# Seven instead of five of sixteen units by Strassen's scheme, with two weight sums made by accumulating transfers

## The chip, the cores and the metric

The kernel runs on one core of a Trainium2 chip. A core has five engines that work side by side, each with its own queue of instructions: TensorE (PE in the profile: matmuls, and PEld: the loads of its stationary operand), VectorE (DVE), ScalarE (ACT), GpSimd (POOL) and SyncE (SP), which here only issues transfers. Sixteen DMA engines carry the transfers. Engines wait for one another through semaphores. Operands lie in SBUF (128 partitions); matmuls write to PSUM, in banks of 128 x 512 float32.

The metric is the time of one execution on the device, in microseconds (us); of several runs the median is taken.

## What is computed

A small encoder of four layers on 256 tokens of width 1024, in float32. Layer i uses token mixer i mod 3: retention, a convolution module, stick-breaking attention, and retention again. After each mixer stands a feed-forward part with the square of a ReLU, and that part is what the change touches:

```python
def squared_relu_mlp(xn, w1, w2):
    h = jax.nn.relu(xn @ w1)
    return (h * h) @ w2

for i in range(DEPTH):              # 4
    ...
    x = x + m                       # m: the mixer of the layer
    x = x + squared_relu_mlp(rms_norm(x, norm_ffn[i]), ffn_w1[i], ffn_w2[i])
return rms_norm(x, final_norm)
```

w1 is 1024 x 4096 and w2 is 4096 x 1024 in each layer. The second product, (h * h) @ w2, is the "second feed-forward product" of this text: 256 tokens, an inner dimension of 4096, 1024 output columns.

## The kernel before

**Products.** Every float32 operand x is split in two: a part hi in the fast matmul type and the rest lo = x - hi. A product a b is three matmuls: a_hi b_hi, a_hi b_lo and a_lo b_hi (`triple`, L687 to L691; its matmul is L689).

**Weights.** All weights come from one array, cut into units of 128 x 1024 and, two units at a time, into chunks of 128 x 2048 (1 MB). `PLAN` (L67 to L107) lists the units in the order of their use. `unit_hi` (L336) loads the next chunk from SP's queue (L348) into one of three `raw` tiles and copies a unit to its hi part on ScalarE (L362, tile `wh`); `unit_lo` (L366) makes the rest on VectorE (L369, tile `wl`). There are five tiles each of `wh` and `wl`. Every unit goes through this conversion, so a chunk's `raw` tile comes free when its last reader is done.

**The second feed-forward product** (`down`, L684). The inner dimension falls into 16 units of 256 rows (kb). For each, the inner 256 rows are two blocks (kk), the tokens are two blocks (t), and the columns are two halves (c); the results stand in four PSUM banks C[t, c]. A plain unit makes all 8 block products, 24 matmuls. The units in `FAST` (L59) use Strassen's scheme in its variant with 7 block products, 21 matmuls. That scheme needs sums on both sides:

- of the activations: s1 to s4, made in `act` (L628, sums at L644 to L646) when the unit's columns of the first product are ready, and split into hi and lo (L652, L653). A unit's sums fill two tiles of 128 x 512. For the first two fast units they lie in `big` tiles, for the other three in `z` tiles, which up to then hold the operand of the first product.
- of the weights: with b11, b21, b12, b22 the four quarters of the chunk, t1 = b11 + b12, t3 = b12 + b22, t2 = t1 + b22 and t4 = t2 + b21. `fast_unit` (L373) makes all four on VectorE (L385), in temporaries (`tmp`, a pool of ten tiles), and converts b22 and the four sums in halves of 512 columns (L392 on ScalarE, L393 on VectorE).

Three of the seven products go to C directly, four to banks of their own (p1, p5, p7, p6; tile `mis`), and after the last mixed unit a few VectorE additions bring these to C.

**Order.** `MIXED` (L60) is the order of the first 12 units: plain and fast ones mixed. `REST` (L61) are the last four units, all plain, first for column half 0 and then for half 1, so that half 0 can be taken out while half 1 is computed. The first product runs over 16 pairs p of 256 columns (`ffn`, L623); pair p becomes the activations of unit kb = p. In the last layer `final` (L829) takes the place of `middle`: it loads the final gain into two `z` tiles (L832) and scales the rows.

Inside most stages the order of instructions on each engine comes from a planner that runs the program against a model of the machine: it gives out the tiles of a pool as they come free, in the order of the instructions that first write them, and puts in the semaphores.

**Other users.** The retention layers (0 and 3) need decay factors, 4 x 384 columns of a constant tile `cst`, loaded from SP's queue in layer 0 while the chunks 6 to 9 are loaded (`DST`, L31, L352 to L354) and used at L1006. GpSimd's queue holds 36 transfers in layer 0 (L898), sums of squares, additions of the convolution layer and a few memsets.

Of the kernel before, what the change touches and what calls it, by code (L numbers as in the profile page):

```python
# [21 lines left out]
RH = 4  # L22
DK = 256
# [7 lines left out]
DST = 6  # L31
# [27 lines left out]
FAST = (5, 6, 13, 14, 15)  # L59
MIXED = (0, 5, 1, 2, 6, 3, 13, 4, 14, 7, 15, 8)  # L60
REST = (9, 10, 11, 12)  # L61
# [48 lines left out]
NCHUNK = NUNIT // UPC  # L110

# [131 lines left out]
class Trunk:  # L243
    def __init__(self, ctx, tc, xT, w, prm, cst, fin, gn, out):
# [24 lines left out]
        self.cst = self.cp.tile([P, NCCOL], F32, name="cst", tag="cst")  # L269
# [66 lines left out]
    def unit_hi(self, key):  # L336
# [3 lines left out]
        if o == 0:  # L340
            n = self.un // UPC
            if n < len(self.first):
                self.rawt = self.first[n]
            else:
                self.rawt = self.raw.tile([P, RAWW], F32, name=self.nm("raw"), tag="raw")
                h = 1024 if n < 4 else UPC * 1024
                for a in range(0, UPC * 1024, h):
                    nc.sync.dma_start(self.rawt[:, a : a + h], self.w_d[n][:, a : a + h])  # L348
            for _ in range(min(2, len(self.later))):
                self.later.pop(0)()  # L350
            i = self.un // UPC - DST
            if 0 <= i < RH:  # L352
                n = CCOL["D"] + i * 384
                self.tc.keep_in_program_order(nc.sync.dma_start(self.cst[:, n : n + 384], self.cst_d[:, n : n + 384]))  # L354
# [18 lines left out]
    def fast_unit(self, name, l, kb):  # L373
        nc = self.nc
        ah, al = self.unit((name, l, "a", kb, 0))
        o = self.un % UPC * 1024
        assert PLAN[self.un] == (name, l, "a", kb, 512) and o
        self.un += 1
        b11, b21, b12, b22 = (self.rawt[:, n * 512 : (n + 1) * 512] for n in range(4))
        t1, t2, t3, t4 = (self.tmp() for _ in range(4))  # L380
        out = [(ah[:, :512], al[:, :512]), (ah[:, 512:], al[:, 512:])]
        h = None
        for n, (dst, x, y) in enumerate(((None, b22, None), (t1, b11, b12), (t3, b12, b22), (t2, t1, b22), (t4, t2, b21))):
            if dst is not None:
                nc.vector.tensor_add(dst, x, y)  # L385
            else:
                dst = x
            if n % 2 == 0:
                h = self.wp.tile([P, 1024], F32R, name=self.nm("wh"), tag="wh")
                g = self.wp.tile([P, 1024], F32R, name=self.nm("wl"), tag="wl")  # L390
            c = slice(n % 2 * 512, (n % 2 + 1) * 512)
            nc.scalar.copy(h[:, c], dst)  # L392
            nc.vector.tensor_sub(g[:, c], dst, h[:, c])  # L393
            out.append((h[:, c], g[:, c]))
        return out
# [227 lines left out]
    def ffn(self, i, nxt):  # L623
        nc = self.nc
        last = nxt is None
        h, rb, fast = [], [], {}

        def act(ps):  # L628
# [12 lines left out]
            if p in FAST:  # L641
# [5 lines left out]
                n = 2 * FAST.index(p) - 4  # L647
                hi, lo = (
                    self.bigt(F32R) if n < 0 else self.zp.tile([P, 512], F32R, name=self.nm("z"), tag=f"z{n + o}")
                    for o in range(2)  # L650
                )
# [32 lines left out]
    def down(self, i, h, fast, begin, hook):  # L684
# [51 lines left out]

        if i == 0:
# [91 lines left out]
    def final(self, i, h, fast):  # L829
        nc = self.nc  # L830
        self.table("sqrt_and_others")
        gain = [self.zp.tile([P, 512], F32, name=self.nm("gain"), tag=f"z{6 + c}") for c in range(2)]  # L832
        for c in range(2):
            nc.sync.dma_start(gain[c], self.fin_d[:, c * 512 : (c + 1) * 512])
# [11 lines left out]
        def hook(C, at):  # L846
            if at:
                return
# [53 lines left out]
    def retention(self, j, nxt):  # L902
# [72 lines left out]
        for h in range(RH):  # L975
# [27 lines left out]
            for t, (c0, c1) in enumerate(((0, S), (S, S + P))):  # L1003
                nc.vector.scalar_tensor_tensor(
                    out=a[t], in0=ps[:, c0:c1], scalar=ck[:, t * 4 + h : t * 4 + h + 1],
                    in1=self.c("D", c1 - c0, h * 384 + c0), op0=ALU.mult, op1=ALU.mult,  # L1006
# [751 lines left out]
```

## Time and profile before

| | |
|---|---|
| median of three runs | 1330.02 us (1329.91 to 1332.01) |
| the profiled execution: time / span | 1329.23 us / 1327.5 us |
| granted TensorE clock | 1.00 |
| TensorE busy, matmuls / weight loads | 1316.6 / 1133.6 us |
| VectorE / ScalarE / GpSimd busy | 1063.9 / 860.1 / 154.1 us |
| moved by DMA | 253.95 MB, 191 GB/s on average |

The span runs from the first to the last instruction of the profiled execution; the rest of its time lies around it. "Busy" is the sum of the listed durations of an engine's instructions. In the rows of the profile, L689 is line 689 of the kernel, an arrow stands between output and input tiles, and "<-ACT wh L362" names what ended a wait. SPq and POOLq are the queues of transfers issued by SP and GpSimd; "us to landing" is the time from a transfer's issue to its end.

The layers' feed-forward parts lie at 178 to 386 us (layer 0), 460 to 664, 750 to 957 and 1117 to the end; in each, the first product takes some 115 us and the second some 80.

### The profile page before, as it was taken

To read this page: it belongs to the slowest core of one execution; us is meant where nothing else is said; L and a number is where in the kernel's file an instruction comes from. 1 tells how busy PE (TensorE), PEld (TensorE's weight loads), DVE (VectorE), ACT (ScalarE), POOL (GpSimd) and SP (SyncE) were. 2 spreads that over 40 slices of the span, in tenths; PEclk is the share of its full clock that TensorE was granted. 3 is DMA by queue.
4 is the path that set the end of the run, shared out by engine and by line. 5 is a ranking of instruction groups with operands and counts; after the bars stand their busy time and mean duration, and the time that the engine had idled before them with its cause. 6 is when DMAs were issued, how large, how long until landed. Compare 5 with 4: busy or idle time off the path is not lost.

```text
span 1327.5 us, 20237 instructions
## 1 busy us (share of the span) xinstructions
PE 1316.6 (99%) x7703; PEld 1133.6 (85%) x7703; DVE 1063.9 (80%) x1805; ACT 860.1 (65%) x1407; POOL 154.1 (12%) x169
## 2 busy tenths in 40 slices
PE   9999999999999999999999999999999999999998
PEld 8988888888899898888888898888888888888886
DVE  7987877779778688798788588798798776798985
ACT  7555546886566478766668678866675555567663
POOL 3554411000009110000000010000020000100000
PEclk9999999999999999999999999999999999999999
DMA  8666655545765655545453355555454554555552
GB/s 312 211 218 223 227 206 191 190 159 201 277 240 152 202 182 193 188 161 220 158 189 130 127 193 189 190 190 210 169 193 171 189 180 160 206 202 191 177 192 94
DMA packets 46049, 253.95 MB, mean 191 GB/s; under 512 B 5376, under 2 KB 10112, under 8 KB 18560
## 3 DMA queue, kind: packets, MB, share of 16 engines
q1 hardware_dynamic: 43360, 245.32, 52.4%
q0 software_dynamic: 1728, 4.72, 0.9%
q10 hardware_dynamic: 864, 2.62, 0.6%
q8 instruction: 60, 0.98, 0.3%
q14 instruction: 37, 0.30, 0.1%
HBM read 245.99 MB, written 6.65 MB: 190 GB/s over the span
## 4 chain that ended last, share of the span: by engine, by line
PE 96%; DVE 2%; ACT 1%; DMA 0%; issue 0%
PE acc L577 22%; PE acc L689 19%; PE acc L573 11%; PE acc L1107 6%; PE acc L1109 6%; PE acc L1108 6%; PE mis L689 3%; PE acc L557 3%; PE acc L558 3%; PE acc L559 3%; PE mis L577 2%; PE acc L1275 1%; PE mis L573 1%; PE acc L1408 1%; DVE wl L393 1%; DVE t L385 1%
## 5 line engine op out<-in xcount | busy, mean ns | idle before, releaser
L369 DVE TENSOR_TENSOR wl<-raw,wh 128x1024 fp32r<-128x1024 f32 (+1 forms) x420 | 512.5, 1231 | 122.1 <-ACT wh L362 119.1
L362 ACT CAST wh<-raw 128x1024 fp32r<-128x1024 f32 (+1 forms) x420 | 433.2, 1041 | 232.4 <-PE acc L689 68.6
L577 PE MATMUL acc<-z,wh 128*128 128x512 f32 x1152 | 399.4, 393 | 0.0
L573 PE MATMUL acc<-z,wl 128*128 128x256 f32 x1152 | 317.6, 280 | 0.0
L689 PE MATMUL acc<-wh,big 128*128 128x512 f32 x800 | 255.9, 391 | 0.0
L577 PEld LDWEIGHTS acc<-z,wh 128*128 128x128 f32 x1152 | 214.2, 187 | 47.1
L573 PEld LDWEIGHTS acc<-z,wl 128*128 128x128 f32 x1152 | 216.9, 189 | 2.4 <-DVE t L602 0.3
L689 PEld LDWEIGHTS acc<-wh,big 128*128 128x128 f32 x800 | 150.2, 188 | 30.7
L689 PE MATMUL acc<-wl,big 128*128 128x512 f32 x400 | 156.2, 390 | 0.5 <-DVE wl L369 0.5
L1107 PE MATMUL acc<-wh,z 128*128 128x512 f32 x352 | 138.6, 394 | 0.0
L1109 PE MATMUL acc<-wh,z 128*128 128x512 f32 x352 | 137.3, 390 | 0.0
L1108 PE MATMUL acc<-wl,z 128*128 128x512 f32 x352 | 137.2, 390 | 0.0
L601 ACT COPY t<-acc 128x256 f32<-128x256 f32 x154 | 53.1, 371 | 57.3 <-PE acc L577 55.4
L689 PEld LDWEIGHTS acc<-wl,big 128*128 128x128 f32 x400 | 75.1, 188 | 17.6 <-DVE wl L369 1.8
L1107 PEld LDWEIGHTS acc<-wh,z 128*128 128x128 f32 x352 | 66.1, 188 | 15.2 <-issue 2.2
L1109 PEld LDWEIGHTS acc<-wh,z 128*128 128x128 f32 x352 | 66.1, 188 | 14.8 <-issue 0.8
L1108 PEld LDWEIGHTS acc<-wl,z 128*128 128x128 f32 x352 | 66.1, 188 | 13.3
L602 DVE TENSOR_TENSOR t<-acc,t 128x256 f32<-128x256 f32 x154 | 59.7, 419 | 17.9 <-ACT t L601 16.0
L392 ACT CAST wh<-t 128x512 fp32r<-128x512 f32 x80 | 47.1, 619 | 35.2 <-DVE t L385 12.3
L557 PE MATMUL acc<-z,wh 128*128 128x256 f32 x224 | 63.7, 284 | 0.0
L492 POOL TENSOR_TENSOR t<-t,t 128x512 f32<-128x512 f32 x15 | 24.2, 1612 | 339.1 <-ACT t L487 308.7
L558 PE MATMUL acc<-z,wh 128*128 128x256 f32 x224 | 63.4, 283 | 0.0
(300 smaller groups left out, 2098.6 us busy)
## 6 DMA issues: line engine op xcount, KB each, us to landing
raw<-in_w SPq DMA_DIRECT2D x214, 1024.0 KB, 4.9
strip<-st POOLq DMA_DIRECT2D x36, 128.0 KB, 4.0
big<-strip SPq DMA_DIRECT2D x18, 256.0 KB, 5.9
big<-in_gn SPq DMA_DIRECT2D x16, 256.0 KB, 5.3
raw<-in_w SPq DMA_DIRECT2D x7, 512.0 KB, 7.4
raw<-hd SPq DMA_DIRECT2D x8, 263.0 KB, 5.2
raw<-hd SPq DMA_DIRECT2D x8, 131.5 KB, 3.6
wh<-in_w ACTq DMA_DIRECT2D x2, 512.0 KB, 6.3
```

The source lines that it names most:

```text
L362: nc.scalar.copy(hi[:, s], src[:, s])
L369: self.nc.vector.tensor_sub(lo[:, s], src[:, s], hi[:, s])
L557: nc.tensor.matmul(o, wh[:, kk, cs], ah, start=st, stop=False, **kw)
L558: nc.tensor.matmul(o, wh[:, kk, cs], al, start=False, stop=False, **kw)
L573: mm = nc.tensor.matmul(ps[m][:, :S], wl[:, kk, cs], a[:, :S], start=first and kk == 0, stop=False, **kw)
L577: nc.tensor.matmul(ps[m], wh[:, kk, cs], a, start=False, stop=last and kk == 3, **kw)
L601: nc.scalar.copy(o[:, s], ps[m][:, S:])
L602: nc.vector.tensor_add(o[:, s], ps[m][:, :S], o[:, s])
L689: mm = nc.tensor.matmul(o, l, r, start=start and n == 0, stop=stop and n == 2, skip_group_check=True)
L1107: nc.tensor.matmul(ps[t], zh[:, s], wh[:, kk], start=k == 0, stop=False, skip_group_check=True)
L1108: nc.tensor.matmul(ps[t], zh[:, s], wl[:, kk], start=False, stop=False, skip_group_check=True)
L1109: nc.tensor.matmul(ps[t], zl[:, s], wh[:, kk], start=False, stop=k == 7, skip_group_check=True)
```

## The change

Units 9 and 12 become fast, so that 7 of 16 units use the scheme; the order of the twelve mixed units is new, with 9 next to 12 and 13 next to 14, and the last four are 7, 8, 10 and 11.

In `fast_unit` two of the four weight sums are no longer made by VectorE. SP's queue loads b12 a second time, into a temporary (t3). GpSimd's queue then issues two transfers that add what they bring to what stands at their destination: b11 onto the chunk's own b12, which makes t1 in place, and b22 onto t3. VectorE still makes t2 and t4. Since t1 and b22 are now next to each other in the chunk, they are converted together, as 1024 columns.

The activation sums of seven units need room: the third pair of tiles takes over the place of the decay factors (`room`, the same tag as `decay`), the other four take all eight `z` tiles. So the decay factors leave `cst` for a tile of their own and are loaded a second time in layer 3, and the final gain is loaded into `big` tiles, after the additions that follow the mixed units.

```diff
-FAST = (5, 6, 13, 14, 15)
-MIXED = (0, 5, 1, 2, 6, 3, 13, 4, 14, 7, 15, 8)
-REST = (9, 10, 11, 12)
+FAST = (5, 6, 9, 12, 13, 14, 15)
+MIXED = (0, 5, 1, 6, 2, 9, 12, 3, 13, 14, 4, 15)
+REST = (7, 8, 10, 11)
...
+DECAY = [PLAN.index(u) // UPC + n for u in (PLAN[DST * UPC], ("ret_w_in", 1, "b", 0, DK)) for n in range(RH)]
...
-            i = self.un // UPC - DST
-            if 0 <= i < RH:
-                n = CCOL["D"] + i * 384
-                self.tc.keep_in_program_order(nc.sync.dma_start(self.cst[:, n : n + 384], self.cst_d[:, n : n + 384]))
+            if self.un // UPC in DECAY:
+                i = DECAY.index(self.un // UPC) % RH
+                if i == 0:
+                    self.decay = self.cp.tile([P, RH * 384], F32, name=self.nm("decay"), tag="decay")
+                n = i * 384
+                self.tc.keep_in_program_order(
+                    nc.sync.dma_start(self.decay[:, n : n + 384], self.cst_d[:, CCOL["D"] + n : CCOL["D"] + n + 384])
+                )
...
     def fast_unit(self, name, l, kb):
         nc = self.nc
-        ah, al = self.unit((name, l, "a", kb, 0))
+        n = self.un // UPC
+        hi, lo, src, cuts = self.unit_hi((name, l, "a", kb, 0))
         o = self.un % UPC * 1024
         assert PLAN[self.un] == (name, l, "a", kb, 512) and o
         self.un += 1
-        b11, b21, b12, b22 = (self.rawt[:, n * 512 : (n + 1) * 512] for n in range(4))
-        t1, t2, t3, t4 = (self.tmp() for _ in range(4))
-        out = [(ah[:, :512], al[:, :512]), (ah[:, 512:], al[:, 512:])]
-        h = None
-        for n, (dst, x, y) in enumerate(((None, b22, None), (t1, b11, b12), (t3, b12, b22), (t2, t1, b22), (t4, t2, b21))):
-            if dst is not None:
-                nc.vector.tensor_add(dst, x, y)
-            else:
-                dst = x
-            if n % 2 == 0:
-                h = self.wp.tile([P, 1024], F32R, name=self.nm("wh"), tag="wh")
-                g = self.wp.tile([P, 1024], F32R, name=self.nm("wl"), tag="wl")
-            c = slice(n % 2 * 512, (n % 2 + 1) * 512)
-            nc.scalar.copy(h[:, c], dst)
-            nc.vector.tensor_sub(g[:, c], dst, h[:, c])
+        _, b21, t1, b22 = (self.rawt[:, i * 512 : (i + 1) * 512] for i in range(4))
+        d11, _, d12, d22 = (self.w_d[n][:, i * 512 : (i + 1) * 512] for i in range(4))
+        t2, t3, t4 = (self.tmp() for _ in range(3))
+        nc.sync.dma_start(t3, d12)
+        nc.gpsimd.dma_start(t1, d11, accum_op=ALU.add)
+        nc.gpsimd.dma_start(t3, d22, accum_op=ALU.add)
+        self.unit_lo((hi, lo, src, cuts))
+        nc.vector.tensor_add(t2, t1, b22)
+        bh, bl = (self.wp.tile([P, 1024], F32R, name=self.nm(t), tag=t) for t in ("wh", "wl"))
+        nc.scalar.copy(bh, self.rawt[:, 1024:2048])
+        nc.vector.tensor_sub(bl, self.rawt[:, 1024:2048], bh)
+        nc.vector.tensor_add(t4, t2, b21)
+        out = [(w[0][:, c : c + 512], w[1][:, c : c + 512]) for w, c in (((hi, lo), 0), ((hi, lo), 512), ((bh, bl), 512), ((bh, bl), 0))]
+        for i, t in enumerate((t3, t2, t4)):
+            if i % 2 == 0:
+                h, g = (self.wp.tile([P, 1024], F32R, name=self.nm(t_), tag=t_) for t_ in ("wh", "wl"))
+            c = slice(i % 2 * 512, (i % 2 + 1) * 512)
+            nc.scalar.copy(h[:, c], t)
+            nc.vector.tensor_sub(g[:, c], t, h[:, c])
             out.append((h[:, c], g[:, c]))
         return out
...
+        def spare(n):
+            if n < 4:
+                return self.bigt(F32R)
+            if n < 6:
+                if n == 4:
+                    room.append(self.cp.tile([P, RH * 384], F32R, name=self.nm("room"), tag="decay"))
+                return room[0][:, (n - 4) * 512 : (n - 3) * 512]
+            return self.zp.tile([P, 512], F32R, name=self.nm("z"), tag=f"z{n - 6}")
...
-                n = 2 * FAST.index(p) - 4
-                hi, lo = (
-                    self.bigt(F32R) if n < 0 else self.zp.tile([P, 512], F32R, name=self.nm("z"), tag=f"z{n + o}")
-                    for o in range(2)
-                )
+                hi, lo = (spare(2 * FAST.index(p) + o) for o in range(2))
...
         nc.vector.tensor_add(uq, u, e5)
         nc.vector.tensor_add(C[1, 1], C[1, 1], uq)
+        hook(C, "gain")
...
     def final(self, i, h, fast):
-        gain = [self.zp.tile([P, 512], F32, name=self.nm("gain"), tag=f"z{6 + c}") for c in range(2)]
-        for c in range(2):
-            nc.sync.dma_start(gain[c], self.fin_d[:, c * 512 : (c + 1) * 512])
+        gain = []
...
         def hook(C, at):
+            if at == "gain":
+                for c in range(2):
+                    gain.append(self.bigt())
+                    nc.sync.dma_start(gain[c], self.fin_d[:, c * 512 : (c + 1) * 512])
             if at:
                 return
```

More of the change, by code (lines that the diff above doesn't have):

```diff
@@ L268, in __init__ @@
         self.prm = self.cp.tile([P, NPCOL - NP0], F32, name="prm", tag="prm")
-        self.cst = self.cp.tile([P, NCCOL], F32, name="cst", tag="cst")
+        self.cst = self.cp.tile([P, CCOL["D"]], F32, name="cst", tag="cst")
         self.first = [self.raw.tile([P, RAWW], F32, name=f"raw{n}", tag="raw") for n in range(3)]
@@ L625, in ffn @@
         last = nxt is None
-        h, rb, fast = [], [], {}
+        h, rb, fast, room = [], [], {}, []
+        def spare(n):
[6 more added lines that the diff above has]
+            return self.zp.tile([P, 512], F32R, name=self.nm("z"), tag=f"z{n - 6}")
         def act(ps):
@@ L1005, in retention @@
                     out=a[t], in0=ps[:, c0:c1], scalar=ck[:, t * 4 + h : t * 4 + h + 1],
-                    in1=self.c("D", c1 - c0, h * 384 + c0), op0=ALU.mult, op1=ALU.mult,
+                    in1=self.decay[:, h * 384 + c0 : h * 384 + c1], op0=ALU.mult, op1=ALU.mult,
                 )
```

## The prediction

> **What bounds the kernel now.** I read four views in this order: the page's head, the chain that ended last, the windows over one layer's feed-forward part, and the groups by line.
>
> ```profile
> span 1327.5 us, 20237 instructions
> PE 1316.6 (99%) x7703; PEld 1133.6 (85%) x7703; DVE 1063.9 (80%) x1805; ACT 860.1 (65%) x1407; POOL 154.1 (12%) x169
> PE 96%; DVE 2%; ACT 1%; DMA 0%; issue 0%
> ```
>
> TensorE is busy for all but 10.9 of 1327.5 us, and the chain runs through it for 96%. A change is worth what it takes off TensorE's queue, less any new idle time there. But "busy" overlaps: a 512-column matmul is listed with about 390 ns, and what counts is the pace at which matmuls follow each other. That stands in the chain, in order of time. The columns are start, length, what; the stretch is layer 0's second feed-forward product (L689).
>
> ```profile
> 303.34 1.15 DVE wl L369
> 304.49 0.04 issue
> 304.53 10.96 PE acc L689 x47
> 315.49 0.68 PE mis L689 x3
> ...
> 319.57 6.12 PE acc L689 x27
> 325.69 0.68 PE mis L689 x3
> ...
> 335.89 0.68 PE mis L689 x3
> ```
>
> The reader is to see two things. The pace is 6.12/27 = 0.227 us a matmul. And the short "mis" pieces mark where a fast unit starts: 315.49, 325.69, 335.89, so a fast and a plain unit together last 10.2 us = (21 + 24) x 0.227, without a gap. Only just ahead of 304.53 does the chain leave TensorE: it waits for VectorE's conversions. The windows say how near VectorE is to its limit there (busy us of each engine, clock, share of the DMA engines, GB/s).
>
> ```profile
> core 0: us, PE busy (x) PEld busy (x) DVE busy (x) ACT busy (x) POOL busy (x), PEclk, DMA share, GB/s
> 129.00:172.00 43.00, 43.00 (x216) 36.32 (x215) 36.37 (x64) 22.55 (x36) 19.83 (x26) 1.00 0.62 209
> 178.00:293.00 115.00, 115.00 (x663) 100.97 (x662) 87.99 (x146) 84.44 (x146) 4.99 (x4) 1.00 0.53 188
> 293.00:310.00 17.00, 16.83 (x77) 13.51 (x76) 15.32 (x27) 12.12 (x19) 0.00 (x0) 1.00 0.34 126
> 310.00:332.00 22.00, 22.00 (x99) 18.22 (x98) 20.84 (x30) 13.17 (x18) 0.00 (x0) 1.00 0.60 210
> 332.00:355.00 23.00, 23.00 (x104) 19.02 (x103) 18.43 (x23) 13.66 (x17) 0.26 (x3) 1.00 0.60 220
> 355.00:372.00 17.00, 17.00 (x81) 14.16 (x80) 11.82 (x15) 8.17 (x10) 0.73 (x6) 1.00 1.03 412
> ```
>
> At 310 to 332 us VectorE has 20.84 of 22 us of work, and TensorE still loses nothing; at 293 to 310 it loses 0.17 us. VectorE is the second limit, ScalarE and the DMA engines (0.60) have room, GpSimd is idle. (The first row, from the retention layer, is used further below.)
>
> **The change, part by part.**
>
> **Matmuls removed.** A plain unit is 8 block products of 3 matmuls, a fast one 7. Two more fast units in each of four layers remove 2 x 4 x 3 = 24 matmuls: 24 x 0.227 = **5.4 us**. The granted clock is 1.00 throughout, so the pace should hold.
>
> **Conversions.** The prices, by line (count | busy us, mean ns; the last row is one of the timeline, with its start and length):
>
> ```profile
> L369 DVE TENSOR_TENSOR wl<-raw,wh 128x1024 fp32r<-128x1024 f32 (+1 forms) x420 | 512.5, 1231 | 122.1 <-ACT wh L362 119.1 <-DMA big<-strip 1.5
> L362 ACT CAST wh<-raw 128x1024 fp32r<-128x1024 f32 (+1 forms) x420 | 433.2, 1041 | 232.4 <-PE acc L689 68.6 <-PE acc L1109 66.7 <-PE acc L577 47.9
> L393 DVE TENSOR_TENSOR wl<-t,wh 128x512 fp32r<-128x512 f32 x80 | 52.5, 686 | 3.8 <-ACT wh L392 3.8
> L392 ACT CAST wh<-t 128x512 fp32r<-128x512 f32 x80 | 47.1, 619 | 35.2 <-DVE t L385 12.3 <-PE acc L689 11.3 <-issue 9.7
> L385 DVE TENSOR_TENSOR t<-t,raw 128x512 f32<-128x512 f32 x40 | 27.5, 687 | 0.3
> L644 DVE TENSOR_TENSOR t<-t 128x256 f32<-128x256 f32 x20 | 8.5, 423 | 4.6 <-ACT t L637 4.5
> L653 DVE TENSOR_TENSOR z<-t,z 128x512 fp32r<-128x512 f32 x12 | 8.2, 686 | 0.1
> 298.30 0.29 DVE L645 TENSOR_TENSOR t<-t,t 128x128 f32<-128x128 f32 x1
> ```
>
> VectorE's share of a fast unit was 1.23 + 5 x 0.69 + 4 x 0.69 = 7.4 us; it becomes 2 x 1.23 + 3 x 0.69 + 2 x 0.69 = 5.9. ScalarE's 1.04 + 5 x 0.62 = 4.1 becomes 2 x 1.04 + 3 x 0.62 = 3.9. Over the twelve mixed units of a layer VectorE had 5 x 7.4 + 7 x 2.46 = 54.3 us for 61.9 us of matmuls, and gets 7 x 5.9 + 5 x 2.46 = 53.5 for 60.5. So the two sums handed to the DMA engines pay for the two extra units: VectorE's load hardly moves, it does not free TensorE. In the first product each new fast pair adds 0.42 + 2 x 0.29 + 0.69 = 1.7 us on VectorE and 0.62 on ScalarE; 27 and 30 idle us in 178 to 293 hide them. Without that cover they would cost 2 x 1.7 us a layer, 13.5 us.
>
> At the seam near 300 us VectorE has two adds (1.4 us) less before TensorE's wait: the 0.17 us a layer may go, up to 0.5 us in all; I count nothing.
>
> **The new chain.** t1 = b11 + b12 and t3 = b12 + b22 now come by transfers. For t1 the raw load lands, GpSimd issues the accumulation, it lands. For t3 SP loads b12 into a temporary, that lands, GpSimd issues, it lands. ScalarE's copies of them stand ahead of the next unit's copies (the five wh tiles are dealt out in order), so a late t3 delays the next unit too. On SP the t3 load stands between raw loads and waits for a temporary; on GpSimd the second accumulation waits for t3's load, with the next unit's accumulations and the following layer's few memsets behind it, which are not urgent. No run of before accumulates; the nearest rows bound it (the list of transfers, where the last number is us from issue to landing, and, with its shortest, median and longest in ns, GpSimd's own time for an issue):
>
> ```profile
> raw<-in_w SPq DMA_DIRECT2D x214, 1024.0 KB, 4.9
> strip<-st POOLq DMA_DIRECT2D x36, 128.0 KB, 4.0
> big<-strip SPq DMA_DIRECT2D x18, 256.0 KB, 5.9
> gain<-in_fin SPq DMA_DIRECT2D x2, 256.0 KB, 2.8
> L898 POOL DMA_DIRECT2D strip<-st x14: 539/580/582, 131.5 to 172.9; - x14
> ```
>
> A 256 KB accumulation takes A: at least 2.8 us (the quiet load), at most twice 5.9 = 11.8 (a busy one that passes its bytes twice). I take **A = 5.5**, near the 5.9 of the same size and above GpSimd's 4.0 for half; GpSimd's issue is 0.6 more.
>
> By the Trainium skill, "DMA: Bandwidth & Descriptors", section "Anatomy of one DMA — SWDGE (gpsimd) path", such a transfer costs about 2.0 us plus its bytes over 436 GB/s, an estimated 2.6 us here. The strip row is slower than that page makes it (4.0 against 2.3 for 128 KB), and by the page all waits below would vanish.
>
> How much time is there? SP's queue in time:
>
> ```profile
> 309.12 0.33 SPq L348 DMA_DIRECT2D raw<-in_w  x1
> 313.30 0.33 SPq L348 DMA_DIRECT2D raw<-in_w  x1
> ```
>
> The load at 309.12 is that of the fast unit which starts at 325.69 (it goes out when the unit three before is converted). t1 feeds its fourth product, at 325.69 + 3 x 0.68 = 327.7, after 1.04 + 1.23 us of conversion, so it must land by 325.5: 16.4 us - 4.9 - 0.6 leaves A up to 10.9. t3 feeds the fifth, at 328.4, after 0.62 + 0.69: by 327.1. With its load behind the unit's own raw load (309.45), A may be 327.1 - 309.45 - 5.9 - 0.6 = 11.1. In the two back-to-back pairs (9 then 12, 13 then 14) the t3 load of the second can only take a place one raw load later (313.6), as its temporary is dealt out after the first unit's: A up to **7.0**. With 5.5, all of it is hidden.
>
> The seam is tighter. The first fast unit follows one plain unit:
>
> ```profile
> 289.58 0.63 ACT L635 ACTIVATE t<-t 128x512 f32<-128x512 f32 x1
> 293.56 0.48 PE L689 MATMUL acc<-wh,big 128*128 128x512 f32 x1
> 296.42 0.42 DVE L644 TENSOR_TENSOR t<-t 128x256 f32<-128x256 f32 x1 [1.36 <-ACT t L637]
> ```
>
> Its fifth product is at 293.56 + (24 + 12) x 0.227 = 301.7, so t3 must land by 300.4. Ten temporaries serve all; with four fast pairs at the end of the first product, I read that t3 gets one that pair 14 used, free when L635 has read it, at 290.2. Then 290.2 + 2.8 + 0.6 + 5.5 = 299.1, or 302.2 if the load takes 5.9: between 1.3 early and 1.8 late. I take 0.3 us a layer, **1.2 us**.
>
> **The rest at nothing.** Four more 192 KB decay loads in layer 3, and the gain load after the last mixed unit, whose user comes after 16 block products x 3 x 0.227 = 10.9 us against 2.8 to land. The sums after the mixed units lose a plain unit of cover but their user has the same 10.9 us. DMA engines: the last window moves 412 GB/s when full. Twelve 1 MB loads are 30.5 us, seven t3 loads 4.5, and fourteen accumulations at twice their bytes 18, together 53 of 60.5 us: not the bound, unless one accumulation costs over 1.8 us of all sixteen.
>
> **Sum.** Profiled execution 1329.2 (span 1327.5 and 1.7 around it) - 5.4 + 1.2 = 1325.0; it ran 0.8 us under the median of 1330.0, so against that median: **1325.8 us**.
>
> **The rivals.**
>
> *Short waits eat the gain* (within 0.2%, which is 2.7 us and about what a measurement can tell from no change). Three places a layer are tight, the seam and two pairs; 0.25 to 0.7 us at each of the 12 is 3 to 8 us: about 1329.5. For it: the seam's sum is within 2 us of its limit. Against: VectorE was 95% busy at 310 to 332 and TensorE lost nothing.
>
> *t3's temporary comes late at the seam* (the other side). If the load has to wait for the temporaries of pair 15, first written at 296.4, t3 lands at 296.4 + 2.8 + 0.6 + 4.0 to 296.4 + 5.9 + 0.6 + 5.9, that is 3.4 to 8.4 us late, in four layers 14 to 34 us: 1338 to 1358, about 1345. It decides from an issue after 291.5 us. For it: those temporaries are all in use just there. Against: ten of them, and SP runs ahead of VectorE.
>
> *Accumulating is dear.* At A = 11.8 the two pairs are 4.8 us late each and the seam about 6 (5.0 to 8.1): 15.6 us a layer, 1387. For it: nothing in the trace shows an accumulation. Against: the engines have 40% free.
>
> *VectorE holds up GpSimd's issue.* If each issue waits for one VectorE instruction (up to 1.23 us), t3 is 2.5 us later: 1.0 late at two pairs and about 2.5 at the seam, 18 us in four layers: 1343. Against: L898's fourteen issues in 131 to 173 us took 0.54 to 0.58 us each, with VectorE 85% busy (36.37 of 43 us). [...]
>
> **How the numbers follow.** Forecast 1325.8, chance 0.50, its own range 1322.5 (the seam's 0.5 gone too, and no wait) to 1327.3. Short waits 0.20. Late temporary 0.15, dear accumulation 0.10, held-up issue 0.05: slower 0.30 together. The range runs from 1322.5 to 1348: it leaves out the dear accumulation and a third of the late temporary.
>
> **What would show it.** Right: L689 with 24 matmuls fewer, TensorE's idle time near 11 us, fast units 4.8 us apart back to back, VectorE's L385 group halved per unit. A late t3 would show as ScalarE's half-width copy waiting for a DMA and as a gap in the chain at a fast unit's fifth product, at the seam first. A dear accumulation would show in its time to landing (over 7 us) and in a DMA share near 1. I am wrong if the pace of a matmul moves, if SP's raw loads get stuck behind a t3 load, or if GpSimd's queue holds the accumulations behind a memset.

## The result and the profile after

The changed kernel is slower: 1373.4 us against 1330.1, a ratio of 1.033 (95% interval 1.030 to 1.037). The forecast was 1325.8, and 1373.4 lies outside its range. The profiled execution took 1372.3 us.

The page of the changed kernel: its head, the chain that ended last, two DMA queues, and the transfers (count, KB each, median us to landing). Its lines have moved: the matmuls are L704, the load of t3 L388, the accumulation onto b12 (t1) L389, that onto t3 L390, the add of t2 L392, of t4 L396.

```profile
span 1370.5 us, 20451 instructions
PE 1331.1 (97%) x7679; PEld 1137.0 (83%) x7679; DVE 1072.7 (78%) x1817; ACT 874.2 (64%) x1419; POOL 207.8 (15%) x225
q0 software_dynamic: 9792, 19.40, 7.5%
PE 79%; DMA 10%; DVE 6%; issue 3%; ACT 2%; POOL 0%; POOLq 0%; ACTq 0%; SPq 0%; DVEq 0%
raw<-in_w SPq DMA_DIRECT2D x214, 1024.0 KB, 4.9
raw<-in_w POOLq DMA_DIRECT2D x28, 256.0 KB, 5.8
t<-in_w SPq DMA_DIRECT2D x28, 256.0 KB, 7.3
t<-in_w POOLq DMA_DIRECT2D x28, 256.0 KB, 6.9
```

The 24 matmuls are gone (7679 for 7703), but the chain runs through TensorE for 79% instead of 96%, and transfers now hold 10% of it. The windows over layer 0's second product have the columns of those shown before:

```profile
293.00:310.00 17.00, 16.89 (x77) 13.62 (x76) 15.75 (x29) 11.09 (x18) 3.58 (x4) 1.00 0.77 200
310.00:332.00 22.00, 19.52 (x84) 15.62 (x83) 12.95 (x15) 11.06 (x14) 4.40 (x5) 0.99 0.98 273
332.00:355.00 23.00, 19.42 (x72) 14.68 (x70) 13.75 (x17) 11.23 (x14) 3.65 (x5) 0.79 0.79 205
355.00:372.00 17.00, 14.09 (x56) 11.31 (x55) 13.02 (x15) 8.82 (x11) 0.25 (x2) 0.90 0.56 176
```

Three things changed at once from 310 us on. TensorE has gaps; VectorE, which had 20.84 of 22 us of work, has 12.95, so it too waits; and the DMA engines are at 0.98 of their time while they move 273 GB/s, where before they moved 412 at 1.03. In the third and fourth window the granted clock is below 1.

From the start of the first to the start of the last matmul the four second products took 85.5, 85.5, 85.5 and 84.4 us before and take 99.1, 94.9, 96.0 and 93.4 now, 42.4 us more in all. The two executions differ by 43.1, so nearly all of it is there. By the starts of the matmuls the 42.4 are: 5.4 less for the matmuls removed, some 36 more of waits and some 11 more of matmuls at half pace, each to a microsecond or two, since a matmul at half pace can also wait.

What the end of the stretch depended on stands in the chain of layer 0, in order of time (start, length, what):

```profile
319.70 7.82 DMA raw<-in_w
...
327.59 0.49 issue
328.08 7.13 DMA raw<-in_w
...
335.23 0.69 DVE t L392
...
340.54 1.15 DVE wl L395
...
341.70 6.72 DMA raw<-in_w
...
348.98 7.25 DMA raw<-in_w
...
358.14 7.13 PE acc L704 x23
365.27 0.68 PE mis L704 x3
```

The reader is to see one figure repeat. A raw load (7.82 us, SP) lands; GpSimd issues; the accumulation makes t1 in that tile (7.13); VectorE adds t2 and t4, works off conversions of other tiles that had queued up (L374, 337.05 to 340.5), and converts t1 and b22 (L395); only then is the tile free, and the load that needs it goes out at 341.70. The chunks at places 8 and 11 of the order, counted from 0, use the same tile, so a turn of the tile took 22.0 us. TensorE works through three chunks with two fast units in 2 x 4.8 + 5.4 = 15.0 us. The last rows show a second loss: after the wait 23 matmuls took 7.13 us, 0.31 each instead of 0.227.

What TensorE itself waits for stands in the timeline (start, length, instruction, and in brackets the idle time before it and what ended that):

```profile
353.00 1.05 ACT L367 CAST wh<-raw 128x1024 fp32r<-128x1024 f32 x1 [0.31 <-PE mis L704]
356.26 0.69 DVE L392 TENSOR_TENSOR t<-raw 128x512 f32<-128x512 f32 x1 [5.25 <-DMA raw<-in_w]
356.87 1.22 DVE L374 TENSOR_TENSOR wl<-raw,wh 128x1024 fp32r<-128x1024 f32 x1
358.14 0.50 PE L704 MATMUL acc<-wl,big 128*128 128x512 f32 x1 [2.91 <-DVE wl L374]
```

VectorE works in the planner's order, and there t2 of the next fast unit stands ahead of conversions that TensorE needs sooner. It stood 5.25 us until unit 15's t1 had landed, and only then converted columns of the plain unit before it, whose chunk had been there since 344.58 and whose copies ScalarE had finished by 354.05. Unit 15 itself starts on TensorE at 365.27. The longest wait of layer 0, 3.89 us until 336.58, is of the same kind: the seventh product of unit 12 needed a conversion that stood behind t2 of unit 13. Of the ten waits of over 1 us in the four second products, 28.6 us in all, eight with 24.5 us end within 3 us behind a t2 that had waited for its t1. The other two are at the fifth product of unit 12, which waits for t3.

### The profile page after: what moved, and what is told of

Its sections match the earlier page's. It is cut to its first block, busy times and chain, and to the rows that moved or that the text cites. A ratio compares the mean times of both kernels' runs of the same rounds, so it can differ in the third digit from the quotient of the medians.

```text
span 1370.5 us, 20451 instructions
## 1 busy us (share of the span) xinstructions
PE 1331.1 (97%) x7679; PEld 1137.0 (83%) x7679; DVE 1072.7 (78%) x1817; ACT 874.2 (64%) x1419; POOL 207.8 (15%) x225
## 4 chain that ended last, share of the span: by engine, by line
PE 79%; DMA 10%; DVE 6%; issue 3%; ACT 2%; POOL 0%; POOLq 0%; ACTq 0%; SPq 0%; DVEq 0%
PE acc L587 19%; PE acc L704 10%; PE acc L583 10%; DMA raw<-in_w 9%; PE acc L1125 6%; PE acc L1127 6%; PE acc L1126 6%; PE acc L567 3%; PE acc L568 3%; PE acc L569 3%; PE mis L587 2%; DVE wl L374 2%; PE mis L704 1%; PE acc L1293 1%; PE mis L583 1%
## 5 line engine op out<-in xcount | busy, mean ns | idle before, releaser
L374 DVE TENSOR_TENSOR wl<-raw,wh 128x1024 fp32r<-128x1024 f32 (+1 forms) x412 | 504.9, 1235 | 120.7 <-ACT wh L367 118.0
L367 ACT CAST wh<-raw 128x1024 fp32r<-128x1024 f32 (+1 forms) x412 | 424.5, 1041 | 213.4 <-PE acc L1127 66.6
L704 PE MATMUL acc<-wh,big 128*128 128x512 f32 x704 | 236.7, 403 | 0.0
L704 PE MATMUL acc<-wl,big 128*128 128x512 f32 x352 | 143.2, 407 | 21.1 <-DVE wl L403 14.9
L704 PEld LDWEIGHTS acc<-wh,big 128*128 128x128 f32 x704 | 137.8, 196 | 28.8
L704 PEld LDWEIGHTS acc<-wl,big 128*128 128x128 f32 x352 | 68.7, 195 | 40.6 <-DVE wl L403 16.9
L389 POOL DMA_DIRECT2D raw<-in_w x28 | 24.6, 880 | 438.4 <-DMA raw<-in_w 289.2
L567 PE MATMUL acc<-z,wh 128*128 128x256 f32 x224 | 63.7, 284 | 0.0
```

The source lines that it names most:

```text
L367: nc.scalar.copy(hi[:, s], src[:, s])
L374: self.nc.vector.tensor_sub(lo[:, s], src[:, s], hi[:, s])
L567: nc.tensor.matmul(o, wh[:, kk, cs], ah, start=st, stop=False, **kw)
L704: mm = nc.tensor.matmul(o, l, r, start=start and n == 0, stop=stop and n == 2, skip_group_check=True)
```

## The experiments

The theory after this reading: the chain of t1 starts only when its chunk has landed and holds the raw tile until it ends, so a late unit makes the load three chunks on late (the ring). The rivals: t3's chain (load, accumulation), the traffic as such, the order of the units, or the room taken by the activation sums. The sum of the four second products, from the profiled execution, stands beside each time (340.9 us for the kernel before, 383.3 for the changed one). The profiled execution of e13 took 1372.3 us, 8.6 above its median, that of e4 5.4 us less than its median; the others lie within 5 us of theirs. Where a kernel makes its sums in a loop over a list, the adds of its edit are written out below.

| kernel | us | ratio to before, 95% interval | second products, us |
|---|---|---|---|
| e1_t1_vectore | 1333.6 | 1.001 (1.000 to 1.003) | 346.5 |
| e2_t3_vectore | 1365.5 | 1.026 (1.023 to 1.029) | 373.1 |
| e3_both_vectore | 1329.7 | 1.000 (0.999 to 1.000) | 339.9 |
| e4_t1_temporary | 1385.3 | 1.041 (1.038 to 1.045) | 390.3 |
| e5_five_units | 1347.3 | 1.012 (1.010 to 1.015) | 359.0 |
| e6_early_release | 1380.9 | 1.037 (1.034 to 1.039) | 394.0 |
| e7_t3_gpsimd | 1344.5 | 1.010 (1.009 to 1.012) | 356.3 |
| e8_t3_ahead | 1331.9 | 1.001 (1.000 to 1.002) | 340.1 |
| e9_seven_later | 1323.5 | 0.994 (0.993 to 0.996) | 333.7 |
| e10_six | 1327.2 | 0.998 (0.997 to 0.999) | 339.9 |
| e11_t1_ahead | 1366.2 | 1.026 (1.025 to 1.028) | 376.2 |
| e12_idle_transfers | 1354.0 | 1.018 (1.016 to 1.020) | 364.9 |
| e13_idle_gpsimd | 1363.7 | 1.025 (1.021 to 1.029) | 381.4 |
| e14_own_queue | 1356.6 | 1.018 (1.015 to 1.021) | 366.7 |
| e15_t1_own_queue | 1343.2 | 1.009 (1.006 to 1.011) | 356.1 |

### Which of the two sums

All three keep the changed kernel's units, order and room.

e1: t1 on VectorE, t3 by transfers. (b22 and the four sums are again converted in halves.)

```diff
-        nc.gpsimd.dma_start(t1, d11, accum_op=ALU.add)
+        nc.vector.tensor_add(t1, b11, b12)
```

> Changed kernel (1373 us), but t1 = b11 + b12 is made by VectorE into a temporary again; t3 still comes by SP's load and GpSimd's accumulation. Ring theory (t1's addition in place holds one of only three raw tiles from its load of 4.9 to 8 us over 0.9 + 5.8 to 7.2 us of accumulation to some 3.5 us of conversion, 16 to 20 us a turn, where TensorE asks for three chunks in 15.0 to 15.6): the hold is gone, 1328 to 1340 us, the rest being VectorE's 6.7 us a fast unit. Theory of t3's chain (7.3 us of load and then 0.9 + 6.9 of accumulation are too long): t3 is as late as before, 1360 to 1375 us. Theory of GpSimd's queue (an accumulation for t1 stands behind one for t3 that waits for its load): nothing is queued behind t3 any more, 1330 to 1340 us.

e2: t1 by accumulation in the raw tile, t3 on VectorE.

```diff
-        nc.sync.dma_start(t3, d12)
-        nc.gpsimd.dma_start(t3, d22, accum_op=ALU.add)
+        nc.vector.tensor_sub(t3, t2, b11)
```

> Changed kernel, but t3 is made by VectorE (as t2 - b11, which is b12 + b22), and only t1 comes by an accumulation in place. Ring theory: the raw tile is held as long as before, 1355 to 1373 us. Theory of t3's chain: the long chain is gone, 1328 to 1340 us. Theory of GpSimd's queue: t1's accumulations no longer wait behind t3's, 1330 to 1342 us.

e3: both edits, so that no sum comes by transfer.

> Seven fast units in the new order, all four weight sums on VectorE, no accumulating transfer. All theories: the transfers' waits are gone; what is left is VectorE with 7 x 7.4 + 5 x 2.46 = 64 us of work a layer for 60.5 us of matmuls: 24 matmuls saved (5.4 us), 2 to 4 us a layer lost, 1331 to 1341 us. If it stays above 1360 us, the order of the units or the place of the activation sums is at fault, not the transfers.

With t3 by transfers alone the time is 1333.6, with t1 alone 1365.5: t1's chain is worth most of the loss, although e2 moves less than e1 (no second load of b12). That rules out t3's chain as the main cause, and e2 also the theory that t1's accumulations stand behind t3's in GpSimd's queue; e3, 1329.7 and even a little under its range, rules out order and room as causes of the 43 us. In e2's list of transfers within 293 to 355 us they look quick, but two of the accumulations in its chain there were not:

```profile
raw<-in_w SPq DMA_DIRECT2D x11, 1024.0 KB, 4.8
raw<-in_w POOLq DMA_DIRECT2D x6, 256.0 KB, 4.0
```

```profile
314.17 7.80 DMA raw<-in_w
...
333.35 8.23 DMA raw<-in_w
```

So e2's median accumulation there is shorter than the 5.5 us of the prediction, and e2 is 35 us slower than before all the same. The median hides two kinds: of the 28 accumulations of the whole execution 12 landed within 4.1 us, and 13, each with other loads under way, took 6.0 to 9.4.

### Freeing the raw tile: three misses

e4 puts t1 into a temporary as well.

```diff
+        nc.sync.dma_start(t1, d12)
         nc.sync.dma_start(t3, d12)
         nc.gpsimd.dma_start(t1, d11, accum_op=ALU.add)
```

> Changed kernel, but t1 too is accumulated in a temporary (SP loads b12 twice, GpSimd adds b11 to the one and b22 to the other), so as many accumulations as before and 7 MB more of loads, and the raw tile is free of them. Ring theory: 1326 to 1340 us. Theory of t3's chain: now two sums have the long chain, 1373 us or more. Theory of GpSimd's queue: 1365 us or more.

A miss: 1385.3. t2 = t1 + b22 and t4 = t2 + b21 still read the raw tile after t1 has come, so by the code it is held until t1 has come, as before. e6 removes that:

```diff
+        nc.scalar.copy(t2, b22)
+        nc.vector.tensor_add(t4, b21, b22)
...
-        nc.vector.tensor_add(t2, t1, b22)
+        nc.vector.tensor_add(t2, t2, t1)
-        nc.vector.tensor_add(t4, t2, b21)
+        nc.vector.tensor_add(t4, t4, t1)
```

> As e4_t1_temporary (t1 and t3 both by a load into a temporary and an accumulation onto it), but nothing that waits for t1 reads the raw tile any more: ScalarE copies b22 to a temporary, VectorE adds b21 + b22 early, and t2 and t4 come from these plus t1. The transfers are the same as in e4, VectorE has one add less in place of none (still two adds a unit), ScalarE one half-width copy more. If the hold of the raw tile is what costs: raw loads go out as early as before the change, 1330 to 1345 us. If the chain load, accumulation, conversion is too long by itself, or the DMA engines are too slow for the extra transfers: 1365 to 1390, like e4.

Again a miss, 1380.9. Its chain and the waits of SP's own queue (us in total, times, longest) say why:

```profile
298.31 7.89 DMA t<-in_w
...
312.16 0.33 SPq L349
...
312.54 8.89 DMA t<-in_w
...
321.98 8.89 DMA t<-in_w
```

```profile
SPq L349 <- DVE wl L374: 23.7, 4, 10.5
SPq L349 <- DVE wl L403: 15.1, 4, 9.9
```

The raw load at 312.16 had waited for a conversion to free its tile, and the loads of t1 and t3 stand behind it in the same queue: they went out at 312.54 and 313.29, and after load and accumulation (8.89 us each for t1) t1 is there at 330.9 and t3 at 334.0. So the chain may end in a tile of its own, but it still begins with the raw loads. Also t1's temporary is now taken for 18 us before t1 is there. e11 was to start earlier: t1 alone by transfers, in a temporary, written one place ahead.

```diff
+                    self.t1[q] = self.tmp()
+                    nc.sync.dma_start(self.t1[q], d12)
+                    nc.gpsimd.dma_start(self.t1[q], d22, accum_op=ALU.add)
```

(The name d22 stands here for the first quarter of the chunk, b11.)

> t1 by a load into a temporary and an accumulation, both written one unit of the order earlier, t3 by VectorE: the counterpart of e2_t3_vectore (1365 us), which makes the same sum with the same number of accumulations, but in the raw tile and only after its load. Theory: what costs is a chain of transfers that starts with the release of a buffer and holds it until its end; here the chain starts early and holds a temporary of its own: 1329 to 1336 us, like e8_t3_ahead. Rival: t1 is needed too early (fourth product, and t2 and t4 after it) for any accumulation: 1350 to 1370.

1366.2, the third miss. Its loads too are in SP's queue behind raw loads (two go out at 307.57, two at 323.64), and VectorE again stands at t2, 4.39 us until 353.29, ahead of TensorE's longest wait of layer 0, 4.94 us. e8 is its counterpart for t3.

> As e1_t1_vectore (t1 by VectorE, t3 by load and accumulation), but t3's temporary is taken and its two transfers are written one unit of the order earlier, so that they go out some 5 us earlier. If e1's remaining loss (1333.6 us) is t3 landing late: 1325 to 1330 us. If it is VectorE's load or the DMA engines' sharing: 1331 to 1336, as e1.

1331.9 with the same traffic as e11, in the range for the case that t3's landing was not the loss. The difference that the code shows: t3 feeds one product and nothing else; t1 feeds an earlier product and also t2 and t4, which read the raw tile and stand in VectorE's order ahead of other units' conversions. No run moves t2 and t4 back in that order, so what this is worth alone stays open.

e5 gives the two transfers to the five units and the order of before.

> The two accumulating transfers stay, but only the five units of before use the scheme, in the order of before. In that order only one pair of fast units stands next to each other in the ring of three raw tiles (positions 1 and 4 of the twelve); in the changed order there are two rows of three (positions 3, 6, 9 and 5, 8, 11). Ring theory (a fast unit's raw tile is held from its load to the landing of t1's accumulation, and the lateness is handed on from turn to turn): 1332 to 1345 us. Rival: every fast unit's accumulations come late by themselves, about 1.5 us for each of the 28 units of the changed kernel, so 20 x 1.5 = 30 us: 1355 to 1365.

1347.3, 2 us above the ring's range and far under the rival's. Of the 18 us that its second products lost, 6.7 and 7.7 fall in the first two layers.

### The traffic

e12 is e3 with the change's transfers added, onto a temporary that nobody reads; in e13 GpSimd issues the load too.

```diff
+        d = self.tmp()
+        nc.sync.dma_start(d, d12)
+        nc.gpsimd.dma_start(d, d11, accum_op=ALU.add)
+        nc.gpsimd.dma_start(d, d22, accum_op=ALU.add)
```

> As e3_both_vectore (1329.7 us; all sums on VectorE), plus the transfers of the changed kernel, one load and two accumulations of 256 KB a fast unit, all onto one temporary that nobody reads. The traffic is that of the change, only nobody waits for it (except the pool of temporaries). If waits on the chain are the cause of the 43 us: 1329 to 1337. If the traffic as such is (the DMA engines are full, raw loads come late): over 1350.

> As e12_idle_transfers, but the load of the idle chain too is issued by GpSimd. In e12's trace SP's queue waited 20.7 us in layer 0 for temporaries that the idle chain held, with the raw loads behind; here only GpSimd's queue can wait for them, and SP's issues raw loads alone. The traffic is the same, 7 loads and 14 accumulations of 256 KB a layer. If waits in SP's queue made e12's 24 us: 1329 to 1338 us. If the traffic as such makes raw loads late: 1345 to 1356.

e12 took 1354.0 us, as expected for the traffic as such, and e13 1363.7, above both of its ranges. Both say that the traffic costs something by itself, and neither gives it pure. In e12 SP's queue waited for temporaries that the idle chain held, with raw loads behind (its waits in layer 0):

```profile
SPq L389 <- DMA t<-in_w: 20.7, 3, 8.0
```

In e13 that is gone, but the idle chains outlast the mixed units, and the work that follows these then waits for a temporary (waits of TensorE and ScalarE, 372 to 398 us):

```profile
PE mis L801 <- ACT t L788: 10.8, 1, 10.8
ACT t L788 <- DMA t<-in_w: 8.8, 2, 8.0
```

These end waits are some 11, 5 and 6 us in three layers, where e3 has next to none. Without them and the half pace behind them, e13's second products sum to about 356, some 16 us over e3's 339.9; as this execution was 8.6 us above e13's median, that is a rough figure. What becomes of raw loads stands in the lists of transfers within 293 to 355 us, first the kernel before, then the changed one, then e13:

```profile
raw<-in_w SPq DMA_DIRECT2D x12, 1024.0 KB, 4.9
```

```profile
raw<-in_w SPq DMA_DIRECT2D x9, 1024.0 KB, 6.7
t<-in_w POOLq DMA_DIRECT2D x7, 256.0 KB, 7.6
raw<-in_w POOLq DMA_DIRECT2D x6, 256.0 KB, 5.8
t<-in_w SPq DMA_DIRECT2D x5, 256.0 KB, 7.3
```

```profile
raw<-in_w SPq DMA_DIRECT2D x10, 1024.0 KB, 7.6
t<-in_w POOLq DMA_DIRECT2D x15, 256.0 KB, 8.2
```

Over the whole execution the median raw load is 4.9 us in all three; within the stretch it goes from 4.9 to 6.7 and 7.6. A median over 214 loads hid it. But long raw loads alone are not the price: in e1, with half of the accumulations, they took 7.3 us in this stretch, and e1 is 3.9 us above e3.

### A chain with its own queue and an earlier start

e14 makes t1 and t3 in temporaries, with all four transfers from GpSimd, two places ahead; e15 only t1.

```diff
+            for q in MIXED[:3] if j == 0 else MIXED[j + 2 : j + 3]:
...
+                    nc.gpsimd.dma_start(t1, d12)
+                    nc.gpsimd.dma_start(t3, d12)
+                    nc.gpsimd.dma_start(t1, d11, accum_op=ALU.add)
+                    nc.gpsimd.dma_start(t3, d22, accum_op=ALU.add)
```

> t1 and t3 both by accumulating transfers, as in the change, but each in a temporary of its own, with its load of b12 issued by GpSimd too and two places of the order ahead of its unit: no part of the chain stands behind a raw load in SP's queue or waits for a raw tile. Theory: the chain is late because it starts no sooner than its unit's raw load, three chunks (15 us) ahead, and takes as long; freed from that it is hidden, and what is left is the cost of the traffic (as e13_idle_gpsimd) and of temporaries held for long: 1330 to 1345 us. Rival: accumulations are too slow or too dear wherever they start: 1355 to 1385, as e4 and e6.

> As e14_own_queue, but only t1 comes by transfers (load of b12 into a temporary and accumulation, both from GpSimd, written two places ahead); t3 is made by VectorE. Seven loads and seven accumulations a layer, the traffic of e1_t1_vectore (1333.6 us), half of e14's (1356.6). Compared with e2_t3_vectore (1365.5, t1 in the raw tile) and e11_t1_ahead (1366.2, t1's load behind raw loads in SP's queue). If t1 costs because its chain starts only with its unit's raw load: 1330 to 1342 us. If t1 by accumulation is late or dear wherever it starts: 1350 to 1370.

e14 is 29 us faster than e4, with the same sums made from the same transfers; 1356.6 lies within the rival's range, at its low end, 12 us above the theory's. e15 took 1343.2, a microsecond over the theory's range, 7 under the rival's, and 22 us under e2 and 23 under e11. It differs from e2 in three things at once, the place of t1, the queue of its load and the start, and no run separates them. Its waits for transfers within 293 to 355 us, and its raw loads there:

```profile
DVE t L392 <- DMA raw<-in_w: 8.9, 3, 4.1
ACT wh L396 <- DMA t<-in_w: 0.6, 1, 0.6
```

```profile
raw<-in_w SPq DMA_DIRECT2D x11, 1024.0 KB, 8.0
```

The wait for t1 has shrunk to 0.6 us. What is left is VectorE's wait of 8.9 us for raw loads, which took 8.0 us there. Their length alone does not explain it, as e1's 7.3 us with the same number of loads and accumulations show; why e15 still takes 13 us more than before stays open.

### Without transfers

e7 lets GpSimd compute t3.

```diff
+        nc.gpsimd.tensor_add(t3, b12, b22)
```

> Seven fast units, no extra transfers; t3 is added by GpSimd in SBUF (the profile of before has such an add of 128 x 512 at 1.6 us), t1, t2 and t4 by VectorE. VectorE's work over the twelve mixed units falls from 64.2 us (e3_both_vectore) to 59.4, under the 60.5 us of matmuls. If VectorE's load is what kept e3 from its gain: 1325 to 1328.5 us. If GpSimd's add slows VectorE's adds down or comes late: 1330 to 1336.

1344.5: above both ranges, and worse than VectorE making all four. GpSimd's add, and VectorE's conversion of b22 (the second row; 685 ns in e3):

```profile
L388 POOL TENSOR_TENSOR t<-raw 128x512 f32<-128x512 f32 x28 | 77.7, 2779 | 460.2 <-ACT t L649 237.4 <-DMA raw<-in_w 88.1 <-ACT z L662 79.2
L398 DVE TENSOR_TENSOR wl<-raw,wh 128x512 fp32r<-128x512 f32 x28 | 23.4, 835 | 0.0
```

Beside a busy VectorE the add takes 2779 ns, while other GpSimd adds of that size in the same kernel (L497) take 1613, and VectorE slows down too. The Trainium skill, "SBUF — State Buffer", section "Who interferes with whom", says that a VectorE instruction with two SBUF inputs contends with a GpSimd instruction that reads SBUF; these rows agree.

e3 had one wait left, 1.0 us at the first fast unit's seventh product in three layers. e9 is e3 in another order, e10 has six fast units.

```diff
-MIXED = (0, 5, 1, 6, 2, 9, 12, 3, 13, 14, 4, 15)
+MIXED = (0, 5, 1, 2, 6, 9, 3, 12, 13, 4, 14, 15)
```

> As e3_both_vectore (seven fast units, all four sums on VectorE, no extra transfers), with another order of the twelve mixed units: 0, 5, 1, 2, 6, 9, 3, 12, 13, 4, 14, 15, so that two plain units follow the first fast one, as in the kernel before. In e3 the trace has one wait of 1.0 us at the first fast unit of three layers, where VectorE is full, and hardly another. If VectorE's backlog at the seam is what took e3's gain, two plain units behind it change nothing at that product itself (it is the unit's own conversions that are late) but let VectorE catch up: 1326 to 1329.5 us. If VectorE's load over the whole stretch (64.2 us of work beside 60.5 of matmuls) decides: 1329.5 to 1333.

> Six fast units (12 is added to the five of before), all sums on VectorE, no extra transfers, the first six places of the order as in the kernel before. 12 matmuls fewer than before, 12 x 0.227 = 2.7 us; VectorE has 6 x 7.4 + 6 x 2.46 = 59.2 us of work beside 61.2 of matmuls. If VectorE's load decides what a further fast unit brings, all of it comes: 1326.5 to 1328.5 us. If the cover at the seam decides, some of it is lost: 1328.5 to 1331.

e9 took 1323.5 us, 2.5 under its range and 0.6% less than the kernel before (ratio 0.994, 0.993 to 0.996), and is the fastest of all. e10 gives 2.8 us, as expected. The wait at the seventh product, which I had expected to stay, is gone: with plain units next, VectorE no longer makes the next fast unit's sums ahead of the first one's. e9's windows and two stretches of VectorE's timeline (start, time to the end of the last, instruction, count):

```profile
293.00:310.00 17.00, 17.00 (x78) 14.13 (x77) 16.30 (x30) 12.71 (x21) 0.00 (x0) 1.00 0.39 133
310.00:332.00 22.00, 22.00 (x98) 18.22 (x98) 21.90 (x32) 13.11 (x20) 0.00 (x0) 1.00 0.65 233
332.00:355.00 23.00, 23.00 (x103) 19.03 (x103) 21.95 (x32) 16.16 (x24) 0.37 (x3) 1.00 0.51 183
```

```profile
325.95 1.22 DVE L374 TENSOR_TENSOR wl<-raw,wh 128x1024 fp32r<-128x1024 f32 x1
327.08 0.68 DVE L397 TENSOR_TENSOR wl<-raw,wh 128x512 fp32r<-128x512 f32 x1
327.69 1.88 DVE L397 TENSOR_TENSOR wl<-t,wh 128x512 fp32r<-128x512 f32 x3
329.49 0.68 DVE L392 TENSOR_TENSOR t<-t,raw 128x512 f32<-128x512 f32 x1
```

By listed durations VectorE is 95 to over 99% busy, and TensorE has not one gap. VectorE's instructions overlap as matmuls do: a half-width one is listed with 0.68 us, but three of them plus the start of the next lie 1.80 us apart, 0.60 each, and the full-width one takes 1.13 of its 1.22. A fast unit made by VectorE alone is therefore 1.13 + 9 x 0.60 = 6.5 us, not 7.4, and a layer's twelve units are 7 x 6.5 + 5 x 2.26 = 57 us beside 60.5 of matmuls. The two sums never had to leave VectorE.

## Why the prediction was wrong

**Matmuls removed.** 24 fewer, as said. "The granted clock is 1.00 throughout, so the pace should hold" did not: where TensorE waited, matmuls ran at half pace afterwards, some 11 us in all. I had named a moving pace as a way to be wrong, but no term stood for it.

**Conversions.** VectorE's load was indeed no bound after the change, but the reading behind it, that seven units need the help, was off: the prices were listed durations, which overlap (e9).

**The new chain** is where the forecast failed, at "How much time is there?". It took the 16.4 us between a load's issue and its unit from the kernel before, as if the change left them alone, and made t1 due only for its own unit's fourth product. Neither held.

The due time came sooner: VectorE reaches t2 earlier in its order and stands there until t1 lands, with other units' conversions behind it. Eight of the ten long waits, 24.5 of 28.6 us, follow such a stop. Unit 15's t1 landed at 356.23, 9 us before its unit began, and TensorE had waited for it all the same.

The lead was shorter, by two ways. In place, the tile's turn is load, issue, accumulation, and then t2, the conversion of t1 and t4, some 0.69 + 1.06 + 1.15 + 0.69 = 3.6 us. With the prediction's own numbers that is 4.9 + 0.6 + 5.5 + 3.6 = 14.6 us against the 15.0 that TensorE leaves: next to no slack, where I counted over 5 us for t1 (A up to 10.9). The turn shown took 22.0: load and accumulation 7.8 and 7.1, and 6.5 from t1's landing to the release. And in SP's queue everything behind a raw load that waits for a tile waits as well, the next raw loads and the loads for t3. Once one unit is late, each later load and accumulation starts late. That the hold of the tile alone costs much is argued, not shown: e6, which frees the tile from what waits for t1, is 4.4 us under e4.

e2 shows the size, 35 of the 43 us with t1's accumulation alone. e15 shows that it is t1's lateness: begun two places ahead, from another queue and in a temporary, the same sum costs 13. How the 22 us between them split into due time, hold and queue stays open.

**Its terms.** A was 5.8 us in the raw tile and 6.9 onto t3, not 5.5: inside the bounds of 2.8 to 11.8. GpSimd's issue took 0.88 us, not 0.6. The load of t3 took 7.3, not 5.9. Those on the way were longer than the medians: in the chains shown of layer 0 accumulations of t1 took 7.1 and 7.3 us in the changed kernel, 7.8 and 8.2 in e2.

**The seam** was right: t3's load for the first fast unit went out at 290.5, as read (290.2), that for the second at 291.8, and the wait at the first one's fifth product is 0.3 us in layer 0 and nothing in the others. The rival of the late temporary did not happen.

**The rest at nothing.** "53 of 60.5 us: not the bound" was too low and the wrong test. The software queue's time (q0, GpSimd's transfers) went from 0.9% of 1327.5 us to 7.5% of 1370.5, some 90 us for 56 accumulations, 1.6 us of all sixteen engines each, not 18/14 = 1.3. With that the sum is 30.5 + 4.5 + 22.4 = 57.4 of 60.5, and the transfers take longer: raw loads 6.7 to 8.0 us in the stretch. The traffic of the change onto a tile that nobody reads costs about 16 us (e13, less its end waits) to 24 (e12, with SP's waits); that overlaps with the chain's 35, and I can't split the 42.4 more finely.

**The rivals.** *Dear accumulation* comes nearest in time (1387) and named a right place, the back-to-back pairs, but with A = 11.8. At unit 12, the second of the first pair, t3's accumulation took 7.9 us against the 7.0 allowed and TensorE waited 2.4 us at the fifth product; that kind of wait is 4.1 of the 28.6 us. Its signs, over 7 us to landing and a DMA share near 1, showed in the stretch (7.6 for t3, 0.98), not in the medians of the whole. *VectorE holds up GpSimd's issue* did not show: all 28 issues onto the raw tile took 0.875 to 0.932 us.

## What to carry to other kernels

When a change puts a transfer between a buffer's load and its release, work out the buffer's whole turn, load to release, and hold it against the time in which the consumer goes once round the ring; a lead read off the old trace is not a given. Where the engine that reads the result works in a fixed order, the result is due when that order comes to its first reader, not when the last user needs it. A transfer that must be early needs a queue in which nothing waits for the buffers that it is to run ahead of. And take an engine's load from the spacing of its instructions where they stand back to back, not from listed durations: a "full" engine may have a tenth to spare.

## What the runs showed of the hardware

- After waits of TensorE the granted clock was 0.5 for 3.4 to 10.2 us at a time, in the changed kernel from 331.6 and 358.9 us in layer 0 and in each later layer; the kernel before shows none within its second products. How long a wait it takes the runs do not fix: in e2 one of 1.95 us was followed by it, in e15 one of 1.98 us was and one of 1.99 us was not. The Trainium skill, "TensorE: Matmul & The Clock Gate", section "Part 1: The HAM clock gate (the "warmup" mystery)", gives half rate after an idle window of about 3.4 us and full rate after a busy one; the lengths agree, the shortest wait is under a window.
- An accumulating transfer of 256 KB held the sixteen DMA engines for 1.6 us, two and a half times the 0.64 that the same bytes take at the 412 GB/s of the plain loads. In e2 those that landed within 4.1 us took the same 1.6 to 1.7, so it is not the crowding.
- GpSimd's own time for issuing an accumulation was 0.88 us against 0.57 for a plain one.
